# A hybrid decoder block on one core: front, retention and MLP entry in another order

## The chip, the core and the metric

The kernel runs on one core of one Trainium2 chip. The metric is the device time of one execution in microseconds; the times given are medians over several runs. TensorE multiplies (PE, with its weight loads as PEld), VectorE (DVE) and ScalarE (ACT) work element by element, GpSimd (POOL) does small things here, and SyncE (SP) issues nearly all transfers, in order.

## What is computed

One block over 1024 rows of width 1024, in float32:

```python
h = rms_norm(x, g_mix)
qa, ka, va, qr, kr, vr, gr, gate_a, gate_r = split(h @ w_in)
ya = rms_norm(diff_attention(qa, ka, va, lam), g_diff_sub) * (1 - lam_init)  # 8 heads, causal
yr = silu(gr) * rms_norm(retention(qr, kr, vr), g_ret_sub)                   # 4 heads, chunks of 128
mixed = sigmoid(gate_a) * (ya @ w_branch_diff) + sigmoid(gate_r) * (yr @ w_branch_ret)
x = x + mixed @ w_out
x = x + square(relu(rms_norm(x, g_mlp) @ w_ff1)) @ w_ff2
x = x + sigmoid(rms_norm(x, g_ple) @ w_ple_gate) * (p @ w_ple)
out = rms_norm(x, g_final)
```

## The kernel before

Every product is made of float32r parts: split (L119) writes a rounded high part with ACT and the rest with DVE, and three matmuls (high x high, high x low, low x high) go into one PSUM bank. The large projections use a seven-product scheme on 2 x 2 blocks: sums of weight blocks (b11, b21, t1 to t4, b22) meet sums of activation blocks (a11, a12, a22, s1, s2o, s3, s4). unit_prep (L264) is a generator that loads a unit's weights and makes and splits their sums in four steps; product (L299) and product_n (L306) are twelve matmuls each.

Buffers in SBUF go by tags (T0 to T7, S0 to S11, wh, wl, raw, Ga, Gb, o, sq, s2), each with one to three buffers; a new tile of a tag waits until the last reader or writer of the old one is done, a store included. PSUM has eight banks: mm 2, qk 3, sm 2, po 1. A planner orders the instructions of each engine at compile time; the program's order gives the priority. Besides, the program keeps a queue of generators: fill(n) (L213) lets the first one run n steps (six matmuls in a gate or branch), so that independent products lie between dependent ones; drain runs them all.

The stages in order:

- Front. Rows of x are loaded (load_x0, three raw buffers), normed (norm_row), turned by TensorE (row_turned) and split; first_half (L401) takes rows 0 to 3, second_half (L408) rows 4 to 7, where sums of blocks are made too. Between the rows lie the first products of V for attention and retention (v_first, L474, evacuated through the tile s2 by v_spill, L462) and pe_steps (L433), which computes p @ w_ple and stores it in pe_d. v_prep (L483) and v_rest (L505) do the other products of V.
- Twenty units give q and k of both branches and silu(gr), with in_prep (L637) as their unit_prep.
- Retention: for each of four heads ret_qk, ret_kn, ret_scores, ret_chain (eight chunks, one after the other) and ret_turn (L804). One gate's products (gate_steps, L689, 16 steps) lie between, and the queue is drained after each head.
- Attention: 64 tiles (att_tile, L928) of scores, softmax, transposes (turn) and weighing, with PLAN's number of filler steps each: four more gates, the retention's branch products, and at last the first products of the other branch (diff_half). LAST steps follow.
- Output product, rows of x1 and the norm before the MLP: the first 512 columns of all rows, then the other 512 row by row, each row normed, turned and split (lines 1066 to 1133). Here this is called the entry.
- First MLP product: 16 units (ff1_prep, L1142, seven products each) whose outputs and sums go to u_d. Second: PAIRS of products with eight banks, then one pair alone with four banks, while rows are normed for the last stage.
- Last stage: the gate of the per-layer input for two column halves, eight rows each; pe is loaded from pe_d, multiplied and added, then the final norm.

## Time and profile before

| what | value |
|---|---|
| time, median of 3 runs | 1977.43 us (1975.87 to 1980.52) |
| the profiled execution's own time | 1982.06 us |
| its span, first to last instruction | 1980.3 us |
| busy: TensorE, DVE, ACT, POOL | 96%, 66%, 44%, 5% |
| granted TensorE clock, mean | 0.989 |
| DMA | 351.76 MB, 178 GB/s mean |

A busy share is an average over stages with different limits. Matmuls are pipelined, so their durations overlap, and a full stretch is better judged by how many of them it holds. The rows further below show stretches and groups.

### The profile page before, as it was taken

The numbers are of one execution on the slowest core, as the hardware profiler recorded it, in microseconds if no ns is written. First come the engines' busy times: TensorE is split into PE (matmuls) and PEld (weight loads), VectorE is DVE, ScalarE is ACT, GpSimd is POOL, SyncE is SP. The second block draws the span as 40 slices with busy tenths as digits, with TensorE's granted clock in tenths as the row PEclk, the third lists the DMA queues.
The fourth block names the chain that finished last, engine by engine and source line by source line (L and its number), as shares of the span: only waits on it lengthen the run. The fifth ranks groups of instructions, "written<-read, shape, count | busy, mean of one in ns | idle before, by whom it ended". The sixth has DMA issues, their size and how long they took to land.

```text
span 1980.3 us, 24252 instructions
## 1 busy us (share of the span) xinstructions
PE 1906.2 (96%) x8976; PEld 1569.8 (79%) x8976; DVE 1307.5 (66%) x2055; ACT 875.9 (44%) x1385; POOL 96.4 (5%) x112
## 2 busy tenths in 40 slices
PE   8999999999998999999998999799999999999998
PEld 6777788888887878787876887688888878888886
DVE  4777765543466578888886534877677676685754
ACT  6533444334444367666664313433333343333533
POOL 0200000000000011111110000000000000000000
PEclk9999999999999999999998999899999999999999
DMA  8644655532756775588624542254454896563513
GB/s 272 218 157 150 204 174 168 185 118 85 258 195 202 241 195 144 158 267 234 165 92 137 181 149 96 75 176 149 143 172 127 319 375 239 204 232 107 181 38 122
DMA packets 244342, 351.76 MB, mean 178 GB/s; under 512 B 16000, under 2 KB 127744, under 8 KB 242944
## 3 DMA queue, kind: packets, MB, share of 16 engines
q1 hardware_dynamic: 244224, 350.22, 54.9%
q8 instruction: 70, 1.15, 0.2%
q14 instruction: 48, 0.39, 0.1%
HBM read 239.54 MB, written 110.62 MB: 177 GB/s over the span
## 4 chain that ended last, share of the span: by engine, by line
PE 71%; DVE 12%; DMA 7%; ACT 4%; issue 3%; POOL 2%; SPq 1%; POOLq 0%; DVEq 0%; ACTq 0%
PE mm L303 17%; PE qk L303 13%; PE qk L1232 6%; PE mm L186 3%; PE mm L188 3%; PE mm L187 3%; PE mm L1232 3%; PE sm L1232 3%; PE mm L201 2%; PE qk L860 2%; PE mm L202 2%; PE mm L200 2%; PE po L1232 2%; PE mm L311 2%; DVE wl L123 2%
## 5 line engine op out<-in xcount | busy, mean ns | idle before, releaser
L186 PE MATMUL mm<-T,wh 128*128 128x512 f32 x384 | 152.6, 397 | 0.0
L188 PE MATMUL mm<-T,wl 128*128 128x512 f32 x384 | 152.0, 396 | 0.0
L187 PE MATMUL mm<-T,wh 128*128 128x512 f32 x384 | 152.0, 396 | 0.0
L867 ACT ACTIVATE S<-S,stat 128x256 f32<-128x256 f32 (+7 forms) x128 | 98.8, 774 | 36.3 <-DVE stat L862 34.6
L123 DVE TENSOR_TENSOR S<-T,S 128x1024 fp32r<-128x1024 f32 (+1 forms) x46 | 64.7, 1415 | 66.4 <-ACT S L122 66.4
L860 PE MATMUL qk<-S,S 128*128 128x512 f32 (+3 forms) x384 | 101.2, 363 | 2.4 <-DVE stat L862 1.9
L230 POOL TENSOR_TENSOR stat<-stat,mhalf 128x1 f32<-128x1 f32 (+1 forms) x28 | 24.4, 872 | 1437.3 <-DVE stat L228 1437.3
L303 PE MATMUL qk<-T,S 128*128 128x512 f32 x384 | 92.7, 390 | 0.0
L303 PE MATMUL mm<-T,raw 128*128 128x512 f32 x384 | 92.2, 389 | 0.0
L122 ACT CAST S<-T 128x1024 fp32r<-128x1024 f32 (+1 forms) x46 | 54.7, 1203 | 81.4 <-PE qk L303 54.7
L303 PE MATMUL mm<-wh,S 128*128 128x512 f32 x256 | 86.0, 397 | 4.3 <-ACT S L122 4.3
L303 PEld LDWEIGHTS qk<-T,S 128*128 128x128 f32 x384 | 72.4, 188 | 15.1
L303 PEld LDWEIGHTS mm<-T,raw 128*128 128x128 f32 x384 | 72.1, 188 | 15.0
L186 PEld LDWEIGHTS mm<-T,wh 128*128 128x128 f32 x384 | 72.5, 189 | 12.7 <-DVE Ga L991 0.4
L188 PEld LDWEIGHTS mm<-T,wl 128*128 128x128 f32 x384 | 72.3, 188 | 12.9
L187 PEld LDWEIGHTS mm<-T,wh 128*128 128x128 f32 x384 | 72.3, 188 | 12.4
L123 DVE TENSOR_TENSOR S<-sm,S 128x512 fp32r<-128x512 f32 (+2 forms) x116 | 64.4, 571 | 26.2 <-ACT S L122 25.5
L122 ACT CAST S<-S 128x512 fp32r<-128x512 f32 (+2 forms) x52 | 48.3, 950 | 60.7 <-PE qk L303 26.5
L862 DVE CUSTOM_DVE_ANT_0 S<-qk,Gb 128x512 f32<-128x512 f32 (+3 forms) x128 | 72.2, 582 | 3.7 <-ACT Gb L849 2.1
L860 PEld LDWEIGHTS qk<-S,S 128*128 128x128 f32 x384 | 61.4, 189 | 16.3 <-DVE stat L862 10.4
L122 ACT CAST S<-sm 128x512 fp32r<-128x512 f32 (+2 forms) x116 | 54.4, 496 | 44.6 <-PE sm L887 35.0
L122 ACT CAST wh<-S 128x1024 fp32r<-128x1024 f32 (+2 forms) x48 | 54.7, 1158 | 42.6 <-PE po L1232 19.6
(335 smaller groups left out, 4832.0 us busy)
## 6 DMA issues: line engine op xcount, KB each, us to landing
T<-in_w_ff SPq DMA_DIRECT2D x56, 512.0 KB, 5.7
S<-in_w_in SPq DMA_DIRECT2D x52, 512.0 KB, 5.0
S<-qk_d SPq DMA_DIRECT2D x96, 256.0 KB, 5.2
S<-in_w_ff SPq DMA_DIRECT2D x40, 512.0 KB, 6.2
qk_d<-T SPq DMA_DIRECT2D x32, 512.0 KB, 2.9
u_d<-S SPq DMA_DIRECT2D x16, 1024.0 KB, 5.2
u_d<-S SPq DMA_DIRECT2D x16, 768.0 KB, 7.0
T<-u_d SPq DMA_DIRECT2D x24, 512.0 KB, 4.5
```

The lines of the kernel that those rows point to most:

```text
L122: nc.scalar.copy(out=hi, in_=src)
L123: nc.vector.tensor_tensor(out=lo, in0=src, in1=hi.bitcast(F32), op=ALU.subtract)
L186: nc.tensor.matmul(out=ps, lhsT=wh(kt), rhs=ah, start=(kt == 0), stop=False)
L187: nc.tensor.matmul(out=ps, lhsT=wh(kt), rhs=al, start=False, stop=False)
L188: nc.tensor.matmul(out=ps, lhsT=wl(kt), rhs=ah, start=False, stop=(kt == KT - 1))
L200: nc.tensor.matmul(out=ps, lhsT=ah, rhs=wh(kt), start=(kt == 0), stop=False)
L201: nc.tensor.matmul(out=ps, lhsT=ah, rhs=wl(kt), start=False, stop=False)
L303: nc.tensor.matmul(out=ps, lhsT=x[:, k, :], rhs=y[:, k, :], start=(first and k == 0 and n == 0), stop=(k == 3 and n == 2), skip_group_chec ...
L860: nc.tensor.matmul(out=ps, lhsT=qs[:, c, qsl], rhs=kk[:, c, k0:k0 + kw], start=(m == 0), stop=(m == 1))
L862: nc.vector.tensor_tensor_reduce(out=pr[:, c, k0:k0 + kw], in0=ps, in1=bias[0][:, S - w + k0:S - w + k0 + kw], scale=-1.0, scalar=mx[:, 2 ...
L867: nc.scalar.activation(out=pc, in_=pc, func=AF.Exp, scale=-1.0, bias=mx[:, 2 * c + n:2 * c + n + 1], accum_out=z[:, c:c + 1])
L1232: nc.tensor.matmul(out=ps, lhsT=a[x][:, m, k, st * P:(st + 1) * P], rhs=b[y][:, m, k, :], start=(g == 0 and k == 0 and n == 0), stop=(g == ...
```

## The change

The parts, in the program's order:

- pe_steps and pe_d go. The first halves (rows 0 to 3) of gates 4 and 5 are computed in the front as early_gate; their second halves stay in the retention. x rows are loaded ahead of b21; the first products of V take the banks qk, qk, qk, po; rows, products and filler steps stand in another order; va's first two weight sums are made before v_rest (ready).
- in_prep keeps its sums in S2 rather than S3, and b11, b21 in wh.
- Retention: the four gates (48 steps) are queued at once and drained after the last head; the next head's q and k are loaded before ret_scores; ret_turn writes f to o and sq in turn and the high parts to Gb.
- Attention: PLAN and LAST differ, and one filler step may go between the two score groups of a tile.
- Entry: both column halves of w_out are loaded at once; each row gets both halves, is stored to x1_d whole and normed while another half row is multiplied (row_half, row_norm, row_turn). Two of the row's sums go to POOL; s3 and s4 are split once for all rows. The first two products of units 0 and 1 (unit_begin) come before the others, and the weight sums' steps move by one (prep_step). Tags differ throughout, and uy has one buffer.
- The pairs of the second MLP product use other tags. p and w_ple are loaded, turned and split in the last pair's second step, and p @ w_ple is computed in the last stage, six matmuls ahead of each row's product.

```diff
-PLAN = ((2, 2, 2, 2, 2, 2, 2, 2),) * HA
-LAST = 16
+PLAN = ((2, 2, 2, 2, 2, 2, 1, 3),) * (HA - 1) + ((2, 2, 2, 2, 2, 2, 2, 8),)
+LAST = 10
...
-        raw = slot(raw_tag)
+        raw = slot(raw_tag, bufs=2 if raw_tag[0] == "w" else 1)
...
-    pn = slot("T6").rearrange("p (c e) -> p c e", e=DPLE)
-    nc.sync.dma_start(out=pn, in_=t["p"][0, 0].rearrange("(c p) e -> p c e", p=P))
+    load_x0(2)
     b21 = load_b("S1", C_VA, 4)
-    wp = slot("T7")
-    nc.sync.dma_start(out=wp.rearrange("p (k n) -> p k n", k=2), in_=w_block(t["w_ple"][0], 0, D, 0, 2))
-    load_x0(2)
...
-    def pe_steps():
-        wph, wpl = [slot(s, F32R).rearrange("p (k n) -> p k n", k=2) for s in ("S10", "S11")]
...
+    def early_gate(g, raw_tag, tags):
...
         yield
...
+        for u in range(2):
+            yield from t_steps([[a11, a12]], 0, lambda kt: w[0][:, kt, u * P:(u + 1) * P],
+                               lambda kt: w[1][:, kt, u * P:(u + 1) * P],
+                               lambda ps: gate_out(2 * g + u, 0, AF.Sigmoid, ps))
+    def gate_out(unit, half, func, ps):
+        o = slot("Ga", F32, (P, HALF), bufs=2)
+        nc.scalar.activation(out=o, in_=ps, func=func)
+        nc.sync.dma_start(out=gt_d[:, unit, hs(half)], in_=o)
...
-        nw = next(prep)
+        w, nw = ready or [next(prep), next(prep)]
...
-    queue.append(pe_steps())
+    early = [early_gate(4, "T6", ("S6", "S9")), early_gate(5, "T7", ("S10", "S11"))]
+    for g in early:
+        next(g)
+        queue.append(g)
...
     def va_first(i):
-        pb[i] = bank()
+        pb[i] = bank(("qk", "qk", "qk", "po")[i])
         v_first(pb[i], p1a, i, w11)
...
     w21 = split_b(b21)
-    fill(3)
-    v_first(pb[0], p1a, 0, w21, va_d)
     first_half(2)
     va_first(1)
-    fill(3)
+    v_first(pb[0], p1a, 0, w21, va_d)
+    first_half(3)
+    b11 = load_b("S0", C_VR, 0)
+    va_first(2)
     v_first(pb[1], p1a, 1, w21, va_d)
-    first_half(3)
-    b11, b21 = load_b("S0", C_VR, 0), load_b("S1", C_VR, 4)
-    va_first(2)
-    fill(2)
     va_first(3)
-    fill(2)
+    norm_row(4)
     v_first(pb[2], p1a, 2, w21, va_d)
+    b21 = load_b("S1", C_VR, 4)
     a22, s1, s2o = op_tiles("T6", "T7"), op_tiles("S7", "S8"), op_tiles("S4", "S5")
-    norm_row(4)
+    w11 = split_b(b11)
+    fill(4)
+    v_first(pb[3], p1a, 3, w21, va_d)
     second_half(4)
-    w11 = split_b(b11)
-    v_first(pb[3], p1a, 3, w21, va_d)
-    fill(3)
     for st in (5, 6, 7):
         norm_row(st)
+    fill(2)
+    p1r = wide("S3")
+    ps = [bank(("qk", "qk", "qk", "po")[i]) for i in range(4)]
+    va = v_prep(C_VA)
+    v_first(ps[0], p1r, 0, w11)
+    v_first(ps[1], p1r, 1, w11)
     second_half(5)
-    p1r = wide("S3")
     w21 = split_b(b21)
-    va = v_prep(C_VA)
-    for i in range(0, 4, 2):
-        ps = [bank(), bank()]
-        for j in range(2):
-            v_first(ps[j], p1r, i + j, w11)
-        fill(1)
-        second_half(6 + i // 2)
-        for j in range(2):
-            v_first(ps[j], p1r, i + j, w21, vr_d)
-        fill(1)
+    fill(2)
+    for i in (2, 3):
+        v_first(ps[i], p1r, i, w11)
+    second_half(6)
+    fill(2)
+    for i in (0, 1):
+        v_first(ps[i], p1r, i, w21, vr_d)
+    fill(2)
+    second_half(7)
+    next(va)
+    for i in (2, 3):
+        v_first(ps[i], p1r, i, w21, vr_d)
     drain()
-    next(va)
     s3, s4 = op_tiles("S6", "S9"), op_tiles("S10", "S11")
+    ready = []
     for f, (hi, lo) in ((f12, s4), (f11, s3)):
+        ready.append(next(va))
         for k in range(0, 4, 2):
             split(f[:, k:k + 2, :], hi[:, k:k + 2, :], lo[:, k:k + 2, :])
     vr = v_prep(C_VR)
-    v_rest(va_d, p1a, va, lambda: next(vr))
+    v_rest(va_d, p1a, va, lambda: next(vr), ready)
...
-        return unit_prep(w_in, *units[n][0:2], ("S1", "S0")[n % 2], "S3", ("S2", "wh", "wl"))
+        return unit_prep(w_in, *units[n][0:2], ("S1", "S0")[n % 2], "S2", ("wh", "wl", "wh"))
...
+            his = slot("Gb", F32R, (P, 1024)).rearrange("p (a s) -> p a s", a=2)
...
-                f = slot("o", F32, (P, HALF))
+                f = slot(("o", "sq")[half], F32, (P, HALF))
...
-                hi = slot("sq", F32R, (P, HALF))
-                split(f, hi, f.bitcast(F32R))
-                for i, d in enumerate((hi, f.bitcast(F32R))):
+                split(f, his[:, half, :], f.bitcast(F32R))
+                for i, d in enumerate((his[:, half, :], f.bitcast(F32R))):
                     move(yr_d[:, i, h * 2 + e, hs(half)], d)
...
         for c in range(2):
+            if c:
+                fill(between)
...
-            scores(b + 1)
+            m = int(n > 1 and (b + 1) % ST > 3)
+            scores(b + 1, m)
+            n -= m
...
-    gates = iter((4, 5, 6, 7, 0, 1, 2, 3))
+    for g in (4, 5, 6, 7):
+        queue.append(gate_steps(g, AF.Sigmoid, (1,) if g < 6 else (0, 1)))
...
-        queue.append(gate_steps(next(gates), AF.Sigmoid))
         if h == 0:
-            fill(4)
+            fill(2)
...
+        if h + 1 < HR:
+            qk = ret_qk(h + 1)
+            tmp = next(qk)
         sT, rfs = ret_scores(h, qd, kd)
         if h + 1 < HR:
-            v1, qk = ret_v(h + 1), ret_qk(h + 1)
-            tmp = next(qk)
+            v1 = ret_v(h + 1)
...
-        drain()
+    drain()
...
-    wq = [load_quad(w_out, quad, 0) for quad in range(2)]
...
-        run(n_steps(mixed, st, lambda kt: wq[kt // 4][0][:, kt % 4, :], lambda kt: wq[kt // 4][1][:, kt % 4, :], ps))
-        nc.vector.tensor_tensor(out=xa, in0=ps, in1=xa, op=ALU.add)
-        nc.sync.dma_start(out=x1_d[:, st, 0:HALF], in_=xa)
...
+    wq = [[load_quad(w_out, quad, n0, tags[2 * quad:2 * quad + 2] if tags else None) for quad in range(2)]
+          for n0, tags in ((0, None), (HALF, ("S0", "S6", "S7", "S8")))]
...
-    f11, f12 = [slot(s).rearrange("p (k s) -> p k s", k=4) for s in ("S3", "S4")]
-    for st in range(ST):
...
+    f11, f12 = wide("S9"), wide("S10")
+    rows, xns = {}, {}
+    def row_half(st, n):
+        if st not in rows:
+            rows[st] = raw_tile()
+            nc.sync.dma_start(out=rows[st], in_=x_d[st * P:(st + 1) * P, :])
+        ps = bank("qk")
+        run(n_steps(mixed, st, lambda kt: wq[n][kt // 4][0][:, kt % 4, :],
+                    lambda kt: wq[n][kt // 4][1][:, kt % 4, :], ps))
+        add(rows[st][:, hs(n)], ps, rows[st][:, hs(n)])
...
+        row = rows.pop(st)
+        nc.sync.dma_start(out=x1_d[:, st, :], in_=row)
+        xns[st] = slot("Gb", F32, (P, 1024))
         ss = stat()
...
-        f21, f1, f2 = small512("o"), small512("sq"), small512("Ga", 2)
+        f21, f1 = small512("o"), small512("sq")
...
+        add(f1, pt[1], f21)
+        put(f1, s1)
+        add(f1, f1, f11[:, :, cs], ALU.subtract)
+        put(f1, s2o)
         put(pt[1], a22)
-        nc.vector.tensor_tensor(out=f1, in0=pt[1], in1=f21, op=ALU.add)
-        nc.vector.tensor_tensor(out=f2, in0=f1, in1=f11[:, :, cs], op=ALU.subtract)
-        put(f2, s2o)
-        put(f1, s1)
-        nc.vector.tensor_tensor(out=f11[:, :, cs], in0=f11[:, :, cs], in1=f21, op=ALU.subtract)
-        put(f11[:, :, cs], s3)
-        nc.vector.tensor_tensor(out=f12[:, :, cs], in0=f12[:, :, cs], in1=f2, op=ALU.subtract)
-        put(f12[:, :, cs], s4)
+        add(f11[:, :, cs], f11[:, :, cs], f21, ALU.subtract, nc.gpsimd)
+        add(f12[:, :, cs], f12[:, :, cs], f1, ALU.subtract, nc.gpsimd)
...
+    row_half(0, 1)
+    row_half(0, 0)
+    for st in range(4):
+        row_norm(st)
+        row_half(st + 1, 0)
+        row_turn(st)
+        if st < 3:
+            row_half(st + 1, 1)
+    a22, s1, s2o = op_tiles("T0", "T1"), op_tiles("T2", "T3"), op_tiles("S11", "S3")
+    row_half(5, 0)
+    row_half(6, 0)
+    row_half(4, 1)
+    row_norm(4)
+    row_half(7, 0)
+    row_turn(4)
+    row_half(5, 1)
+    row_norm(5)
...
+    def prep_step(u):
+        if u >= UNITS:
+            return
+        if u not in preps:
+            preps[u] = unit_prep(w1, u * P, DFF // 2 + u * P, "wl", "T4", ("wh", "T5", "T6"))
+        opsof[u] = next(preps[u])
+    def unit_begin(u):
...
+        ux = slot(("T7", "S9")[u % 2]).rearrange("p (i s) -> p i s", i=4)
+        pa, pb = bank(), bank("qk")
+        p1 = slot("Ga", F32, (P, HALF), bufs=2)
+        product(pa, ops["b11"], a11, True)
+        nc.scalar.copy(out=p1, in_=pa)
+        product(pb, ops["b21"], a12, True)
+        add(ux[:, 2, :], pb, p1)
+        relu2(ux[:, 2, :])
+        begun[u] = pa, ux
...
-    def ff1_prep(u):
-        return unit_prep(w1, u * P, DFF // 2 + u * P, ("T4", "T5")[u % 2], "T6", ("T7", "S3", "S4"))
...
-    nxt = ff1_prep(0)
-    for _ in range(4):
-        ops = next(nxt)
+    prep_step(0)
+    row_half(6, 1)
+    row_turn(5)
+    row_norm(6)
+    prep_step(1)
+    row_half(7, 1)
+    row_turn(6)
+    row_norm(7)
+    unit_begin(0)
+    row_turn(7)
+    s3, s4 = op_tiles("S0", "S6"), op_tiles("S7", "S8")
+    for f, (hi, lo) in ((f11, s3), (f12, s4)):
+        prep_step(0)
+        for k in (0, 2):
+            split(f[:, k:k + 2, :], hi[:, k:k + 2, :], lo[:, k:k + 2, :])
+    prep_step(0)
+    unit_begin(1)
     for u in range(UNITS):
...
-        ux = slot(("S8", "S10")[u % 2]).rearrange("p (i s) -> p i s", i=4)
-        uy = slot(("S11", "S5")[u % 2]).rearrange("p (i s) -> p i s", i=4)
...
+        if u not in begun:
+            unit_begin(u)
+        now, (pa, ux) = opsof.pop(u), begun.pop(u)
+        uy = slot("S10").rearrange("p (i s) -> p i s", i=4)
...
-        product(pa, now["b11"], a11, True)
...
-        add(ux[:, 2, :], pb, p1)
...
-        ops = next(nxt, None)
+        if u:
+            prep_step(u + 1)
...
-    xs = halves(("S3", "S4", "S6", "S7"))
...
+    xs = halves(("S0", "S6", "S7", "S8"))
...
-    hilo = iter((("S0", "S1", "S2", "S9"), ("wh", "wl", "wh", "wl"), ("T0", "T1", "T2", "T3")) * 8)
-    raws = iter((("T4", "T5"), ("T6", "T7"), ("S5", "S8"), ("S10", "S11")) * 6)
+    hilo = iter((("S4", "S5", "S1", "S2"), ("wh", "wl", "wh", "wl"), ("T0", "T1", "T2", "T3")) * 8)
+    raws = iter((("T7", "T4"), ("S11", "S3"), ("T5", "T6"), ("S9", "S10")) * 6)
+    SIDE = ("S4", "S5", "S10", "S11")
...
+        if g == 1:
...
+            pT = [slot(s, F32R).rearrange("p (k s) -> p k s", k=2) for s in ("S9", "S2")]
...
+            wph, wpl = load_pair(t["w_ple"][0], 0, ("S3", "S1"))
...
-            pe = slot(("o", "sq")[st % 2], F32, (P, HALF))
-            nc.sync.dma_start(out=pe, in_=pe_d[:, st, n0:n0 + HALF])
+            pe = bank("qk")
+            mm = [(a[:, k, ss_], w[:, k, n0:n0 + HALF]) for k in range(2)
+                  for a, w in ((pT[0], wph), (pT[0], wpl), (pT[1], wph))]
+            for i, (l, r) in enumerate(mm):
+                nc.tensor.matmul(out=pe, lhsT=l, rhs=r, start=(i == 0), stop=(i == len(mm) - 1))
```

## Rows read from the trace of the kernel before

**Rows 1.** The page, part 1: busy us (share of span) and instructions of each engine.
```profile
PE 1906.2 (96%) x8976; PEld 1569.8 (79%) x8976; DVE 1307.5 (66%) x2055; ACT 875.9 (44%) x1385; POOL 96.4 (5%) x112
```
**Rows 2.** Busy time by stretch: stretch, length, engines' busy us (instructions), granted clock, DMA share, GB/s.
```profile
2.60:76.00 73.40, 68.42 (x323) 56.28 (x324) 46.03 (x57) 46.49 (x79) 10.94 (x12) 0.95 0.81 275
76.00:112.00 36.00, 28.24 (x118) 21.98 (x117) 26.56 (x31) 18.13 (x27) 6.27 (x4) 0.95 0.52 168
112.00:225.00 113.00, 109.11 (x471) 89.05 (x470) 79.30 (x103) 36.24 (x48) 0.00 (x0) 0.98 0.50 167
225.00:521.50 296.50, 296.50 (x1309) 245.51 (x1309) 158.19 (x207) 116.42 (x164) 0.00 (x0) 1.00 0.48 158
521.50:697.00 175.50, 165.54 (x917) 137.96 (x916) 105.72 (x222) 72.82 (x176) 8.82 (x6) 0.99 0.68 221
697.00:1041.00 344.00, 332.62 (x1818) 272.66 (x1817) 290.85 (x700) 237.93 (x462) 51.13 (x61) 1.00 0.64 179
1202.10:1278.80 76.70, 63.64 (x279) 49.45 (x278) 54.37 (x82) 36.47 (x63) 5.52 (x7) 0.91 0.33 100
1570.00:1600.00 30.00, 28.10 (x123) 22.59 (x122) 13.17 (x10) 7.71 (x6) 0.00 (x0) 1.00 0.98 359
1600.00:1972.00 372.00, 371.77 (x1671) 307.77 (x1669) 242.97 (x248) 143.05 (x150) 9.96 (x15) 1.00 0.52 180
```
**Rows 3.** Timeline of TensorE in the entry: start us, us, what [idle before, its end].
```profile
1193.34 0.39 PE L200 MATMUL mm<-S,T 128*128 128x512 f32 x1
...
1203.14 1.07 PE L1104 MATMUL sm<-ident,Gb 128*128 128x128 f32 x8 [0.58 <-DVE Gb L1096]
1203.97 0.48 PE L201 MATMUL mm<-S,T 128*128 128x512 f32 x1
```
**Rows 4.** Groups, TensorE, 76 to 112 us: count, busy us, mean ns, idle before, releaser.
```profile
L311 PE MATMUL mm<-wh,T 128*128 128x512 f32 x32 | 11.8, 438 | 4.4 <-DVE s L123 4.4
L311 PE MATMUL mm<-wh,S 128*128 128x512 f32 x28 | 9.4, 393 | 3.0 <-DVE s L123 3.0
```
**Rows 5.** Timeline of TensorE at the first unit of the input projection.
```profile
215.42 2.88 PE L303 MATMUL qk<-T,S 128*128 128x512 f32 x12
219.81 0.73 PE L303 MATMUL mm<-S,wh 128*128 128x512 f32 x2 [1.51 <-ACT wh L122]
221.07 1.31 PE L303 MATMUL mm<-S,wh 128*128 128x512 f32 x3 [0.53 <-DVE wh L123]
```
**Rows 6.** Retention, 521.5 to 697: two groups of TensorE, then a row of the waits.
```profile
L810 PE MATMUL sm<-ident,S 128*128 128x128 f32 x64 | 11.9, 283 | 4.5 <-DVE S L801 4.2 <-DVE o L813 0.2
L730 PE MATMUL sm<-ident,S 128*128 128x128 f32 x32 | 4.8, 277 | 1.0 <-DVE o L813 1.0
DVE o L813 <- DMA yr_d<-o: 22.4, 8, 4.7
```
**Rows 7.** Groups, TensorE, 1041 to 1062 us, the end of attention.
```profile
L887 PE MATMUL sm<-ident,S 128*128 128x128 f32 x15 | 3.1, 373 | 6.4 <-DVE S L873 6.4
```
**Rows 8.** Groups, TensorE, 1202.1 to 1278.8 us, the entry.
```profile
L303 PE MATMUL mm<-S,T 128*128 128x512 f32 x24 | 8.7, 511 | 4.9 <-DVE T L123 3.2 <-ACT T L122 1.7
L1104 PE MATMUL sm<-ident,Gb 128*128 128x128 f32 x64 | 8.5, 276 | 3.8 <-DVE Gb L1096 3.8
L303 PE MATMUL mm<-wh,S 128*128 128x512 f32 x8 | 4.7, 657 | 4.3 <-ACT S L122 4.3
```
**Rows 9.** Timeline of DVE and POOL in the front, row 5's sums.
```profile
68.53 0.68 DVE L315 TENSOR_TENSOR sq<-sq,T 128x512 f32<-128x512 f32 x1
...
69.35 1.29 POOL L315 TENSOR_TENSOR T<-T,o 128x512 f32<-128x512 f32 x1 [4.64 <-DVE sq L315]
69.89 1.30 DVE L123 TENSOR_TENSOR S<-sq,S 128x512 fp32r<-128x512 f32 x1 [0.69 <-ACT S L122]
70.60 1.75 POOL L315 TENSOR_TENSOR T<-T,sq 128x512 f32<-128x512 f32 x1
```
**Rows 10.** Waits, 1570 to 1600 us: who for what, us in total, times, longest.
```profile
ACT T L122 <- DMA S<-u_d: 16.9, 1, 16.9
```

117 lines of the change are left out of this document (42 added, 75 removed).

## The prediction

> **What bounds the kernel now.** I read the totals of the page first, then one table of busy time by stage, then in each stage with loss the groups of instructions and what ended the idle time before them. TensorE is busy 1906.2 of 1980.3 us [rows 1], so no other engine's work counts except where TensorE waits for it. The table shows where that is [rows 2]. The twenty units of the input projection (225 to 521.5 us) are full: 1309 products of 512 columns in 296.5 us, which prices one at 0.2265 us. Eight transposes take 0.83 us, from 1203.14 to 1203.97, or 0.104 us each [rows 3]. With these two prices a stage's need is its counts, and the rest is loss:
>
> - 2.6 to 76 us: 227 products and 96 transposes (24 of them the warm-up) need 61.4 of 73.4, loss 12.0, which is the start-up.
> - 76 to 112: 110 and 8 need 25.7 of 36, loss 10.3.
> - 112 to 225: 471 products need 106.7 of 113, loss 6.3.
> - retention, 521.5 to 697: 10.0 idle; attention to 1041: 11.4 idle; at its end 6.4 idle in one place [rows 7].
> - the entry into the MLP, 1202.1 to 1278.8: 215 and 64 need 55.3 of 76.7, loss 21.4, a part of it at the lower clock level (granted clock 0.91, the share at 1.2 GHz), after TensorE had stood idle.
> - start of the second MLP product, 1570 to 1600: 123 need 27.9 of 30, loss 2.1.
> - 1600 to 1972 is full again (371.77 of 372).
>
> So at most some 80 us can be had, and only by giving TensorE something to do in those places.
>
> **The change, part by part.**
>
> The PLE product p @ w_ple leaves the front and goes into the last stage. It is 96 products (2 x 6 for each of eight rows) and 16 transposes (four groups of four in pe_steps): 96 x 0.2265 + 16 x 0.104 = 23.4 us. The last stage is full [rows 2], so all of it is added there. In its place two gates' first halves (2 x 2 chains x 24 = 96 products, 21.7 us) come into the front and leave the retention. TensorE's total does not change: front -1.7, retention -21.7, end +23.4. The transfers of pe_d (16 stores, 16 loads) vanish; they were not waited for on the path. I add 1 us at the end for transposes and weight splits put between full products. The nearest row for such a seam is the 0.5 to 0.6 us that TensorE idles ahead of an inserted transpose [rows 3]; bounds 0 (the stage has DVE to spare) and 4 us.
>
> Front, start-up (loss 12.0): the same first row, constants and weights lead, so I count 0. The PLE products did fill the stretch to 76 us; now the rows themselves must, two products of 12 for each row and block, until the gates may start after row 3. Without 1 MB of p and 1 MB of w_ple ahead of them in SP's queue the third and fourth row come earlier. Bounds: 4 us lost, 2 gained.
>
> Front, 76 to 112 (loss 10.3): TensorE waits 4.4 + 3.0 us for DVE's writes into s2 [rows 4], which is one buffer that waits for its own store to land, while only two mm banks hold products. The change puts the first products into the three qk banks and po, spreads rows 5 to 7 between products and has gate steps ready beside them. I take 7 back; bounds 0 and 9.
>
> Front, 112 to 225 (loss 6.3): at 215.42 twelve products begin and should be followed at 218.14; the next come at 219.81 and, after two, at 221.07, waiting for the split of t2 [rows 5]. That is 1.67 + 0.81 us, and some 1.4 us at the lower clock after it. The cause is in the code: in_prep's sums go to S3, which is p1r, read until the last output of v_rest. Now they go to S2, free long before. With the sums of the V part prepared earlier (ready) I take 3.5; bounds 0 and 5.
>
> Retention: 21.7 us of gate products go, 10.0 us of idle stay in my sum, so 0. For a gain: f alternates between o and sq, and DVE's eight waits for the landing of its own store (22.4 us [rows 6]) should shrink; q and k of the next head are loaded before ret_scores. For a loss: there are 48 gate steps rather than 64 to lie between the head's dependent steps, no drain after each head, and hi now lies in Gb, one buffer that ret_chain's rsp also uses. A wait on it would hold ACT, with the gate's sigmoid, the splits of the next head and so TensorE's banks behind it. TensorE's own idle ahead of the transposes (4.5 us, 4.2 of them for the row scale after the chain's end [rows 6]) is not touched. Bounds: 6 lost, 4 gained, before the rival below.
>
> Attention: one filler step goes between the two score groups, and the plan of steps changes from 2 each to 1 and 3 at a head's end, with 8 in the last tile. Sum of steps: 144 before and after. Of 11.4 us idle I take 1.5; bounds 3 lost, 6 gained. At the end those 6.4 us are a wait for the last probabilities [rows 7]; the added steps need the weights of w_branch_diff, which stand behind the same reload in SP's queue, so 0; bounds 3 lost, 4 gained.
>
> MLP entry (loss 21.4). Two parts of it have different cures. First, while rows are finished, the transposes wait a little each [rows 8]: 3.8 us over eight rows. From the end of row 0's products (1193.34 + 24 x 0.2265 = 1198.78) to its transposes at 1203.14 [rows 3] the norm takes 4.4 us. The new order puts 24 other products (5.4 us) ahead of the transposes, which covers 4.4. Second, at the end nothing is left to do while the last row is normed, turned and split: 4.9 + 4.3 us idle ahead of the units' products [rows 8], and their mean of 511 and 657 ns against the 0.39 us of a product in a full stretch [rows 3] shows the lower clock behind it. The new order keeps unit 0's and unit 1's first two products (2 x 24, 10.9 us) for that gap, and loads and splits unit 0's weights ahead of it. What is late next: DVE has row 7's four splits and sums, the t2 split, the s3 split, each before its product; by about 0.68 us for 512 columns [rows 9] that is some 7 us ahead of t2 against 5.4 us of cover, so 2 us lost there, and up to 1 us a row for rows 4 to 7, whose norms share DVE with the splits of the row before. Four rows hold only three raw buffers, so row 7's load waits for row 4's store; hidden, if its bank may stay full meanwhile. I leave 7 of the 21.4, a gain of 14.5; bounds 8 and 18.
>
> Two of the row's sums move to POOL there. In the front the same two take 1.29 and 1.75 us, and a DVE split that fell beside them took 1.30 us, not 0.68 [rows 9]: 0.6 us of DVE, or 1.2 a row, which the 7 us hold. The Trainium skill ("SBUF — State Buffer", section "SBUF: two separate sides") says more: DVE, with two SBUF inputs, and GpSimd lock a shared port pair for a whole instruction, and the loser fully blocks. By that DVE could stand 1.29 + 1.75 us a row, and the last row's share alone would lie on the path: 3.0 us rather than 1.2 of the entry's gain lost. The row bears out the lock, not its full length.
>
> First MLP product: steady at 19 us a unit and full before. uy becomes one buffer; it is written again some 13 us after its store is issued. 0; bounds 3 lost, 0. Second product's start (2.1): the third pair of raw tiles is no longer the last unit's output, whose store held a load for 16.9 us [rows 10]; gain 1.5; bounds 0 and 2.
>
> Sum: 7 + 3.5 + 1.5 + 14.5 + 1.5 - 1 = 27 us. Against the profiled execution's 1982.06 that is 1955; its median of three is 1977.43, so 1950. The bounds taken together (not all at once) make it 1937 to 1963.
>
> **The rivals.**
>
> A. The retention does not shrink. A head takes 175.5 / 4 = 43.9 us now; my sum needs 38.5. If a head is its own chain of dependent steps (scores, eight chunks, row scale, transposes) rather than TensorE's work, the gate products leave and nothing moves, while the 23.4 us at the end are certain. Price 21.7: 1972. For it: DVE and ACT are only 60% and 41% busy there [rows 2], so latency rules. Against: only 10.0 us were idle, and later steps can be drawn into the gaps.
>
> B. Gb becomes the wait, the side on which the kernel is slower. Per head the second e waits for the first's stores and the next head's rsp for the second's, with the alibi load behind the last: some 12 waits. At the 2.8 us mean of today's eight (22.4 / 8 [rows 6]) that is 34 us if all lie bare: 1984. It decides once 10 of the 12 are bare. For it: ACT waits in order. Against: today's 22.4 us left TensorE no more than 1.2 us idle on that tile (0.2 and 1.0 [rows 6]).
>
> C. The entry's new order does little. The program's order is only a priority for the planner, which already put the transposes into the next row's products [rows 3]; if the last rows' DVE chain is the bound, 14.5 us stay: 1965.
>
> **How the numbers follow.** My forecast 0.62, A 0.16, B 0.10, C 0.12. A change within 0.2% (4 us) can't be told from none here. The forecast gives faster 0.61 and same 0.01; A 0.09 faster, 0.05 same, 0.02 slower; B 0.02 same, 0.08 slower; C 0.11 faster, 0.01 same: faster 0.81, same 0.09, slower 0.10. The range 1936 to 1975 holds the forecast's own, C and most of A.
>
> **What would show it.** Retention some 154 us long, with no ACT wait on Gb's stores; entry with under 8 us of loss and no long stretch at 1.2 GHz; 76 to 112 us without waits for s2; no wait for t2 at the first unit; the last stage 23 to 25 us longer and still full. I am wrong if the retention keeps over 170 us, if TensorE idles over 5 us for rows between the start-up and 76 us, or if the MLP's first unit waits for its split as long as before.

## The result: slower, not faster

| kernel | median of the runs | against before, 95% interval | profiled execution | span |
|---|---|---|---|---|
| before | 1980.5 us (5 runs beside the changed kernel) | 1 | 1982.06 us | 1980.3 us |
| changed | 1994.8 us (5 runs) | 1.0074 (1.0055 to 1.0092) | 1991.08 us | 1988.4 us |

The forecast was 1950 us and faster. The page of the changed kernel, part 1, answers [rows 1]: as many TensorE instructions, of the same kinds, as long busy. So what was lost lies between them.

```profile
PE 1905.5 (96%) x8976; PEld 1571.5 (79%) x8976; DVE 1318.1 (66%) x2047; ACT 871.2 (44%) x1371; POOL 108.2 (5%) x120
```

Busy time by stretch answers [rows 2] (same columns; the stretches are cut where the same work begins and ends):

```profile
2.60:76.00 73.40, 69.26 (x324) 56.86 (x325) 52.36 (x64) 47.72 (x77) 16.89 (x14) 0.95 0.78 250
76.00:112.00 36.00, 33.01 (x142) 26.92 (x141) 26.81 (x31) 14.75 (x19) 3.32 (x2) 0.95 0.44 148
203.50:248.70 45.20, 40.73 (x170) 32.79 (x169) 30.17 (x41) 19.50 (x28) 0.00 (x0) 0.92 0.47 161
515.30:652.30 137.00, 127.84 (x738) 108.39 (x736) 96.69 (x199) 63.31 (x155) 7.29 (x4) 0.98 0.72 233
652.30:1020.60 368.30, 352.48 (x1903) 287.90 (x1902) 302.42 (x724) 244.96 (x479) 52.30 (x63) 1.00 0.66 183
1129.90:1262.00 132.10, 120.13 (x546) 97.41 (x545) 72.58 (x91) 43.54 (x68) 17.12 (x16) 0.99 0.28 93
1544.80:1600.00 55.20, 45.59 (x193) 36.96 (x192) 33.22 (x22) 18.01 (x11) 0.00 (x0) 0.91 1.01 381
```

The reader is to see three things. From 76 to 112 us TensorE does 142 instructions where it did 118. The retention (515 to 652 us) is 137 us long rather than 158.7 (521.6 to 680.3 before). And the start of the second MLP product, which was nearly full, has 45.6 us of work in 55.2 and a granted clock of 0.91.

For the sum a stage's loss is counted more finely than in the prediction: for each TensorE instruction the distance to the next start, less the step that its kind takes in full stretches (0.2267 us for 512 columns, 0.173 for 384, 0.120 for 256, 0.104 for 128, 0.060 for the retention's scores). These steps are those at the full clock, so time at the lower clock counts as loss too. In us, from the two profiled executions:

| stage | before | changed | change | forecast |
|---|---|---|---|---|
| to the first unit | 25.2 | 17.8 | -7.4 | -7 |
| first two units | 4.2 | 7.1 | +2.9 | -3.5 |
| other units and retention, to the first scores | 24.6 | 25.1 | +0.5 | 0 |
| attention, to the last scores | 31.3 | 38.2 | +6.9 | -1.5 |
| attention's end | 11.9 | 11.9 | 0 | 0 |
| branch products after it | 1.6 | 3.3 | +1.7 | 0 |
| entry, w_out to the units | 22.6 | 16.6 | -6.0 | -14.5 |
| first MLP product | 0 | 0 | 0 | 0 |
| second product, its first four pairs | 2.5 | 11.7 | +9.2 | -1.5 |
| rest and last stage | 9.6 | 10.1 | +0.5 | +1 |
| sum | 133.4 | 141.6 | +8.2 | -27 |

The sum is the difference of the spans, 8.1 us. Of the row on the rest and the last stage some 8.7 us lie behind TensorE's last product in either kernel. Between the forecast of -27 and these +8.2 lie 35 us: 10.7 in the second product's start, 8.5 in the entry, 8.4 in the attention, 6.4 in the first units, 1.7 in the branch products. The medians differ by more, 14.3 us: the profiled execution is the fastest of the changed kernel's five, with a granted clock of 0.986 in the mean, and the other four, 3 to 5 us longer, have 0.982 to 0.985. A correction to the text ahead: the input projection has sixteen units (eight of the attention, two times four of the retention), not twenty; the price of a product taken from that stretch is not affected.

How far one execution may be trusted shows where the code of a stage is the same in several kernels below. Entry and branch products together lose 19.9 us in the changed kernel's profile and 19.9 to 27.8, mean 24.4, over the seven profiled executions that have that code unchanged; before it was 24.2, and 24 in d_before_front_dve, whose entry is the same. In the mean over the seven the entry alone loses 3.5 us less than before (6.0 in this one execution) and the branch products 3.4 us more, so that the two together gain nothing. The spread goes with the clock: from the attention's end to the units the changed kernel and c_banks_mm have stops of like length (among them 3.0, 3.6, 4.0 and 2.1 us; 3.2, 3.8, 4.0 and 2.1), but the granted clock of that stretch is 0.99 in the one and 0.95 in the other: over 200 us some 2 us are lost by the clock, over 206 us some 10. The other stages are steadier: first two units 6.1 to 8.0 us, attention 37.5 to 38.5, second product's start 11.4 to 14.4, retention 24.6 to 30.4.

### The profile page after: what moved, and what is told of

Same layout as the page of the kernel before. It is cut to its first block, busy times and chain, and to the rows that moved or that the text cites. A ratio compares the mean times of both kernels' runs of the same rounds, so it can differ in the third digit from the quotient of the medians.

```text
span 1988.4 us, 24138 instructions
## 1 busy us (share of the span) xinstructions
PE 1905.5 (96%) x8976; PEld 1571.5 (79%) x8976; DVE 1318.1 (66%) x2047; ACT 871.2 (44%) x1371; POOL 108.2 (5%) x120
## 3 DMA queue, kind: packets, MB, share of 16 engines
q8 instruction: 70, 1.15, 0.2%
## 4 chain that ended last, share of the span: by engine, by line
PE 69%; DVE 12%; DMA 8%; issue 4%; ACT 4%; POOL 2%; SPq 0%; POOLq 0%; DVEq 0%; ACTq 0%
PE mm L302 17%; PE qk L302 12%; PE qk L1264 5%; PE mm L1264 3%; PE sm L1264 3%; PE mm L187 3%; PE mm L185 3%; PE mm L186 3%; PE qk L853 2%; PE po L895 2%; PE po L1264 2%; DVE wl L122 2%; DVE S L122 1%; PE mm L201 1%; PE mm L200 1%
## 5 line engine op out<-in xcount | busy, mean ns | idle before, releaser
L121 ACT CAST wh<-S 128x1024 fp32r<-128x1024 f32 (+1 forms) x60 | 69.2, 1168 | 107.5 <-PE qk L302 34.6
L302 PE MATMUL mm<-S,T 128*128 128x512 f32 x384 | 92.8, 390 | 2.6 <-DVE S L122 1.9
L302 PE MATMUL mm<-S,wh 128*128 128x512 f32 x384 | 92.5, 390 | 0.0
L302 PE MATMUL qk<-S,wh 128*128 128x512 f32 x384 | 92.4, 389 | 0.0
L302 PEld LDWEIGHTS mm<-S,T 128*128 128x128 f32 x384 | 71.9, 188 | 18.7 <-DVE S L122 2.3
L302 PEld LDWEIGHTS qk<-S,wh 128*128 128x128 f32 x384 | 72.1, 188 | 15.0
L302 PEld LDWEIGHTS mm<-S,wh 128*128 128x128 f32 x384 | 71.8, 188 | 15.1 <-ACT o L656 0.2
L122 DVE TENSOR_TENSOR T<-T,T 128x1024 fp32r<-128x1024 f32 (+1 forms) x24 | 37.6, 1578 | 66.9 <-ACT T L121 66.9
L187 PEld LDWEIGHTS mm<-T,wl 128*128 128x128 f32 x352 | 66.6, 189 | 11.7
L895 PEld LDWEIGHTS po<-S,S 128*128 128x128 f32 x480 | 65.0, 194 | 13.4 <-DVE S L122 7.1
L186 PEld LDWEIGHTS mm<-T,wh 128*128 128x128 f32 x352 | 66.4, 189 | 11.3
```

Source lines behind the costliest of these rows:

```text
L121: nc.scalar.copy(out=hi, in_=src)
L122: nc.vector.tensor_tensor(out=lo, in0=src, in1=hi.bitcast(F32), op=ALU.subtract)
L186: nc.tensor.matmul(out=ps, lhsT=wh(kt), rhs=al, start=False, stop=False)
L187: nc.tensor.matmul(out=ps, lhsT=wl(kt), rhs=ah, start=False, stop=(kt == KT - 1))
L302: nc.tensor.matmul(out=ps, lhsT=x[:, k, :], rhs=y[:, k, :], start=(first and k == 0 and n == 0), stop=(k == 3 and n == 2), skip_group_chec ...
L895: nc.tensor.matmul(out=out, lhsT=v[:, k, :], rhs=a[:, k, q0:256], start=(k == 0 and n == 0), stop=(k == nkt - 1 and n == 2))
```

## The experiments

All are against the kernel before on the same chip, run beside it. The changed kernel was not run again: where a run is compared with it, its 1994.8 us and its ratio of 1.0074 are those of the first comparison. The loss is that of the stage for which the run was made.

| run | median, us | ratio, 95% interval | stage loss, changed kernel to this |
|---|---|---|---|
| a_rows_late | 1983.9 | 1.0011 (0.9994 to 1.0027) | second product's start 11.7 to 0.0 |
| a_p1_gb | 1994.8 | 1.0063 (1.0043 to 1.0084) | first two units 7.1 to 3.2 |
| a_plan_before | 1996.2 | 1.0068 (1.0045 to 1.0091) | attention 38.2 to 38.5 |
| b_turn_last | 1993.2 | 1.0054 (1.0033 to 1.0075) | attention 38.2 to 32.6 |
| b_turn_all | 2016.6 | 1.0178 (1.0159 to 1.0197) | attention 38.2 to 52.3, retention 25.1 to 29.8 |
| a_sums_dve | 1989.4 | 1.0038 (1.0025 to 1.0051) | entry 16.6 to 11.9 |
| b_wq_order | 1994.3 | 1.0058 (1.0037 to 1.0079) | entry and branch products 19.9 to 17.4 |
| b_all | 1963.9 | 0.9913 (0.9895 to 0.9931) | all of these |
| c_all_plan | 1965.1 | 0.9937 (0.9920 to 0.9955) | attention 33.1 (b_all) to 33.0 |
| c_banks_mm | 1997.4 | 1.0102 (1.0078 to 1.0127) | to the first unit 17.8 to 18.1 |
| c_all_front_dve | 1957.7 | 0.9895 (0.9879 to 0.9912) | to the first unit 18.0 (b_all) to 13.2 |
| d_before_front_dve | 1971.8 | 0.9958 (0.9945 to 0.9972) | to the first unit 25.2 (before) to 17.3 |

### The second MLP product: a queue

The changed kernel, TensorE's timeline (start, length, what, in brackets the idle time before and its end), then the waits from 1550 to 1566 us (who for what: total, times, longest), then SP's timeline:

```profile
1554.79 1.07 PE L1264 MATMUL po<-S,S 128*128 128x512 f32 x4
1565.47 0.80 PE L1264 MATMUL mm<-wh,wh 128*128 128x512 f32 x1 [9.61 <-ACT wh L121]
```
```profile
DVE S L1282 <- DMA S<-in_w_ff: 12.5, 1, 12.5
```
```profile
1539.57 3.33 SPq L1227 DMA_DIRECT2D S<-x_d  x5
1548.03 0.37 SPq L1218 DMA_DIRECT2D u_d<-S  x1
1549.83 0.37 SPq L1220 DMA_DIRECT2D u_d<-S  x1
1550.26 3.02 SPq L1227 DMA_DIRECT2D S<-x_d  x3
1553.32 1.10 SPq L1234 DMA_DIRECT2D S<-in_w_ff  x2
```

S3, from which the second weight pair is summed, was s2o, whose last reader is among the first products of the last unit; it is free early. But SP issues in order: rows of x1, which waited 4.4 us for TensorE's reads of the last unit's operands, that unit's two stores, three more rows, and only then S3. The edit, after the products of the first block:

```diff
-    for st in range(ST):
-        nc.sync.dma_start(out=xs(st), in_=x1_d[:, st, :])
...
+            if us == (2, 4) and g == 3:
+                for st in range(ST):
+                    nc.sync.dma_start(out=xs(st), in_=x1_d[:, st, :])
```

> The changed kernel with one move: the eight loads of x1 rows (xs) are no longer issued ahead of the second MLP product but after the fourth of its weight pairs, g == 3 of the first block. Nothing is left out. Theory Q (queue): TensorE's 9.6 us stop at the second pair of raw tiles (S11, S3) is SP's queue: five row loads that wait for the last unit's operands, behind them that unit's two stores, behind them three more row loads, and only then the loads of S3, at 1553.3 us. With the rows later, S3 can be loaded while the last unit still runs; the loss of that stretch falls from 11.7 us to 1 to 3, and the kernel is 8 to 10 us shorter (about 1985 where the changed kernel's median is 1994.8). Rival R: S11 and S3 come free too late whatever stands in the queue, or the stores alone hold it: the loss stays above 6 us and the kernel gains less than 4 us, or the rows, now late, make the first block's last sums wait.

Measured: loss 0.0, and a ratio 0.6% lower, 12 us. SP's timeline of a_rows_late shows the load of S3 15 us sooner, ahead of the last unit's stores:

```profile
1537.81 1.17 SPq L1232 DMA_DIRECT2D S<-in_w_ff  x2
...
1550.51 0.37 SPq L1218 DMA_DIRECT2D u_d<-S  x1
1552.32 0.36 SPq L1220 DMA_DIRECT2D u_d<-S  x1
```

Theory Q holds, with more than it promised: the 2.0 us at the lower clock after the stop went as well.

### The first unit: one wait behind another

The changed kernel, TensorE and then ScalarE at the first unit; it answers [rows 5]:

```profile
213.17 0.49 PE L302 MATMUL mm<-T,wh 128*128 128x512 f32 x1 [1.28 <-ACT wh L121]
216.86 0.79 PE L302 MATMUL mm<-S,wl 128*128 128x512 f32 x1 [3.20 <-ACT Ga L650]
```
```profile
216.22 0.59 ACT L650 COPY Ga<-mm 128x512 f32<-128x512 f32 x1 [3.10 <-DMA vr_d<-Ga]
```

The first line is the second unit's first product, which stops 1.3 us for a split of its weights. t2 is the line below it, at 216.86 and not at 213.17 as the expectation says. t2 (mm<-S,wl) no longer waits for its sums; it waits until its bank's first product is copied to p1, and p1 lies in Ga, out of which the V part's last rows are still being stored.

```diff
-        p1 = slot("Ga", F32, (P, HALF), bufs=2)
+        p1 = slot("Ga", F32, (P, HALF), bufs=2) if n else slot("Gb", F32, (P, 1024))[:, HALF:]
```

> The changed kernel with one buffer changed: the first unit's p1 lies in the free half of Gb rather than in Ga. Theory G: t2's product at 213.17 us no longer waits for t2's sums but for the copy of its own bank into p1, and that copy for Ga, which a last row of the V part is still being stored from (ScalarE idle 3.10 us until the landing in vr_d). With another buffer the wait goes: the loss of the first two units falls from 7.1 us to 2 to 4, the kernel is 3 to 5 us shorter, about 1991. Rival H: o, which u2 of that unit uses and which is stored from in the same way, or DVE's order (two splits of the unit's weights ahead of the last rows' sums) holds the unit as long, and no more than 1 us is won.

Measured: 7.1 to 3.2 us; t2 starts at 208.9. The kernel's time can't tell these 4 us (the intervals overlap). The next wait is already there: t4 stops 2.4 us at 222.5, since DVE's sum for its bank stands behind a subtraction that waits 3.6 us for the second unit's weights. Theory G holds, and the lesson is that this is the third wait in a row at the same place.

### The attention: not the plan, but a table and a queue

> The changed kernel with the attention's order of before: two filler steps in every tile, 16 in the last, none between the two groups of scores. Theory T: the 6.9 us that the attention lost against before (38.2 us of TensorE loss rather than 31.3, by my count of starts against 0.2267 us a product) come from this order: fewer steps lie between the scores and the transposes that wait for the probabilities (17.6 us of waits rather than 8.7). Undone, the stretch goes back to 30 to 33 us of loss and the kernel is 5 to 8 us shorter, about 1988. Rival U: the loss comes from what else runs there (other gates in the queue, another phase of the throttle), and stays above 36 us, with the kernel within 2 us of 1994.8.

(The edit restores PLAN, LAST and att_tile of before.) Measured: 38.5, no change. Theory T falls. A count of the filler products (1536 in gates and branches) that remain as each of heads 0 to 4 begins shows another difference. Before: 1152, 1024, 936, 844, 752. Changed: 1152, 1010, 912, 834, 743. With the plan of before: the same as changed, so the program's number of steps does not decide what TensorE takes. The reason stands in the waits from 646 to 676 us:

```profile
DVE S L855 <- DMA Gb<-in_alibi: 9.7, 1, 9.7
```

and in SP's timeline there: the alibi table goes into Gb, so its load waits for the last head's stores out of Gb:

```profile
653.42 0.93 SPq L88 DMA_DIRECT2D yr_d<-Gb  x2
...
659.88 0.40 SPq L88 DMA_DIRECT2D yr_d<-Gb  x1
660.37 0.41 SPq L88 DMA_DIRECT2D yr_d<-sq  x1
662.79 0.33 SPq L838 DMA_DIRECT2D Gb<-in_alibi  x1
```

Meanwhile TensorE took 14 filler products more, which cost little then (head 0 loses 4.5 us, 3.4 before). In head 4 (9.4 us of loss, 5.3 before) they are missing:

```profile
862.49 0.39 PE L187 MATMUL mm<-T,wl 128*128 128x512 f32 x1
863.37 0.63 PE L880 MATMUL sm<-ident,S 128*128 128x128 f32 x4 [0.49 <-DVE S L866]
...
872.10 0.62 PE L853 MATMUL qk<-S,S 128*128 128x384 f32 x2 [1.65 <-DVE stat L855]
...
877.15 0.40 PE L185 MATMUL mm<-T,wh 128*128 128x512 f32 x1
```
```profile
862.59 0.33 SPq L919 DMA_DIRECT2D ya_d<-o  x1
862.96 1.73 SPq L88 DMA_DIRECT2D S<-qk_d  x3
864.78 1.52 SPq L88 DMA_DIRECT2D S<-va_d  x2
866.35 4.51 SPq L985 DMA_DIRECT2D Ga<-gt_d  x2
```

From 862.7 to 877.2 there is no filler: 696 products remain, 29 chains of 24, so a chain has just ended, and the gates that free the mm banks (L985) stand in SP's queue behind a store that waits and the next head's loads. Before, ten products were left at this place. The edit gives the last head's ret_turn its old buffers:

```diff
+            old = h == HR - 1
-                f = slot(("o", "sq")[half], F32, (P, HALF))
+                f = slot("o" if old else ("o", "sq")[half], F32, (P, HALF))
+                hi = slot("sq", F32R, (P, HALF)) if old else his[:, half, :]
```

> The changed kernel with ret_turn of the last retention head on the buffers of before (f in o, hi in sq; the other heads keep hi in Gb). Theory L: the attention's 6.9 us come from Gb: its first scores need the alibi table, which lies in Gb, and its load stands behind the last head's four stores from Gb (DVE idle 9.67 us until it lands at 669.7 us). Meanwhile TensorE takes filler products from the queue, 142 of 512 columns in head 0 rather than 128, and so stands at the end of a chain 9 products sooner in head 4, where the next gate's load is not issued yet (4.2 of the 6.9 us are lost there, 862 to 877 us). With Gb free the alibi table is loaded before the last head's stores, about 128 filler products go into head 0, and the attention's loss falls from 38.2 to 31 to 34 us; the kernel is 4 to 7 us shorter than 1994.8. Rival M: the last turn's own stores and splits (o is one buffer again) hold the attention's start as long, or the place in head 4 does not depend on the number of products taken; the loss stays above 36 us.

Measured: 1028, 934, 844, 752 products remain as heads 1 to 4 begin, as before within four; head 4 loses 5.5 us, the attention 32.6. Theory L holds for the stage, in b_all, c_all_plan and c_all_front_dve too (32.8 to 33.1). This run's own time does not show it (1.0054, and the interval overlaps that of the changed kernel). In its profile the retention lost 30.4 us; b_all, with the same edit, lost 24.8 there, so the edit does not force that loss.

> The changed kernel with ret_turn of all four heads on the buffers of before. It tells what the new buffers are worth in the retention: from the end of the input projection to the first scores the changed kernel loses about 25.1 us, of which 3.3 us wait for ScalarE's writes into Gb. If the new buffers cost there (rival B of the prediction, in small), this stretch is 1 to 4 us better than with the last head alone undone; if they pay (f alternates and no landing of a store is waited for), it is 1 to 4 us worse. The attention as with the last head alone.

Measured: 2016.6 us, 20 us worse than the changed kernel. The first scores begin at 673.0 rather than 652.3 us, and 70 filler products have been drawn into the retention and are missing in the attention. So the new buffers, and not the smaller number of gate products alone, let the retention shrink: with the old ones DVE waits for each store again:

```profile
DVE o L806 <- DMA yr_d<-o: 15.1, 7, 5.4
```

> The five edits together (1963.9 us), and with them the attention's order of before (two filler steps in every tile, 16 in the last, none between the two groups of scores). Alone on the changed kernel this order moved nothing, but there the filler had run ahead. Theory T2: now that head 0 takes its 128 filler products, the order matters: the attention's loss goes from 33.1 to about 31.3, that of before, or less, and the kernel is 2 us shorter. Rival U2: what the program asks for is not what the engines get, since the planner puts steps where its own times leave gaps; the attention stays at 32 to 34 us of loss and the kernel within 2 us of 1963.9.

Measured: 33.0 us, 1965.1: rival U2. The plan is worth nothing in either place, and as many filler products remain at heads 0 to 4 as in b_all.

### The entry: POOL's sums, and quarters in one buffer

DVE in the changed kernel's entry, groups of one shape (count, busy us, mean ns), then DVE and POOL at row 6:

```profile
L122 DVE TENSOR_TENSOR S<-sq,S 128x512 fp32r<-128x512 f32 x4 | 6.0, 1495 | 0.0
L122 DVE TENSOR_TENSOR T<-sq,T 128x512 fp32r<-128x512 f32 x4 | 2.7, 686 | 0.1
```
```profile
1230.36 1.62 POOL L314 TENSOR_TENSOR S<-S,o 128x512 f32<-128x512 f32 x1 [3.27 <-DVE sq L314]
1230.85 1.67 DVE L279 TENSOR_TENSOR T<-wl,T 128x512 f32<-128x512 f32 x1
1231.93 1.74 POOL L314 TENSOR_TENSOR S<-S,sq 128x512 f32<-128x512 f32 x1
1232.44 1.78 DVE L122 TENSOR_TENSOR S<-sq,S 128x512 fp32r<-128x512 f32 x1
```

The mean of S<-sq,S mixes two cases: the three that began beside a POOL sum took 1.75 to 1.78 us, and row 4's, which began after its sums had ended, took 0.68. Seven of the eight POOL sums of the entry find a DVE instruction beside them and lengthen it by 0.8 to 1.1 us. In the timeline above DVE ends 0.54 and 0.55 us after the POOL sum that it met (1232.52 against 1231.98, 1234.22 against 1233.67), although it began 0.5 us after that sum: it stood until POOL was done. The second POOL sum, in turn, ends 1.15 us after the DVE instruction that it met.

```diff
-        add(f11[:, :, cs], f11[:, :, cs], f21, ALU.subtract, nc.gpsimd)
-        add(f12[:, :, cs], f12[:, :, cs], f1, ALU.subtract, nc.gpsimd)
+        add(f11[:, :, cs], f11[:, :, cs], f21, ALU.subtract)
+        add(f12[:, :, cs], f12[:, :, cs], f1, ALU.subtract)
```

> The changed kernel with the two sums a row of rows 4 to 7 in the entry into the MLP on DVE instead of POOL. Theory P: a DVE instruction beside a POOL sum takes 1.7 to 2.3 us where it takes 0.68 to 1.22 alone; eight such lengthen DVE by about 1 us each, four rows by 8 us, while the sums themselves would cost DVE 8 x 0.68 = 5.4 us. So DVE ends the entry some 2 to 3 us sooner and TensorE's loss there falls from 16.6 us to 13 to 15; the kernel 1 to 3 us shorter. Rival V: the entry waits elsewhere (a norm that started late, row 7's chain), and the loss stays within 1 us of 16.6, or grows by up to 3 us as DVE has more to do.

Measured: the entry's loss is 11.9, below all seven executions with that code unchanged (16.6 to 21.7), the kernel 5 us shorter (1.0038 for 1.0074, the intervals apart). Theory P's outcome came, by more than the 2 to 3 us expected. Its sum is not all of it: DVE was lengthened by 7.1 us and took over 5.4, which is 1.7 us. The planner also gives the instructions another order, and what that brought is not isolated.

> The changed kernel with the four quarters of w_out loaded in another order: both quarters of the second half (into S0, S6, S7, S8) ahead of the first half's second quarter. Theory W: the stop of 3.4 us at 1133.8 us waits for the last quarter of the second half, which the first product of the rows needs; it came late since two of the three raw buffers were held by the first half's second quarter, whose split waits for wh and wl until the branch products end (1129.7 us), so that four loads passed through one buffer, 6.2 us each. In the new order they pass through three buffers. The stop goes, the stretch from the attention's end to the unit products loses 2.5 to 4 us less (19.9 us in the changed kernel), the kernel about 1991. Rival X: the first half's second quarter, now last, takes its place: row 0's first half waits for it, or the rows of x come later, and less than 1 us is won.

(The order of load_quad becomes first half's first quarter, second half's two, first half's second.) Measured: w_out's last quarter is loaded at 1119 to 1121 us, not at 1132.7, and the 3.4 us stop is gone; entry and branch products 17.4 us, under the 19.9 to 27.8 of the unchanged ones. Theory W holds in the trace; the time alone can't tell it.

### Together, and the front

> The changed kernel with five edits together: the x1 rows loaded after the fourth weight pair, the first unit's p1 in Gb, the entry's row sums on DVE, ret_turn of the last head on the buffers of before, the quarters of w_out in the new order. If the causes are separate, the gains add: 12 (second MLP product) + 4 (first units) + 5 (entry) + 5 (attention) + 3 (w_out) = 29 us less than 1994.8, about 1966, faster than the kernel before (1981) by 0.6 to 0.9%. If a wait that is removed only passes the time on to the next one, the sum falls short: 1975 to 1985.

Measured: 1963.9 us, 31 us less than the changed kernel. In ratios the five single runs gain 0.63, 0.11, 0.20, 0.36 and 0.16%, together 1.46%, and b_all 1.61%: the gains add, and the causes are separate. By stage, from its profile: second product's start 11.7 us less, first units 2.3, attention 5.1, entry and branch products 11.4 (19.9 to 8.5); together 30.5, and over all stages 30.0 (141.6 to 111.6).

> The changed kernel with the V part's first products in the two mm banks, as before, rather than in the three qk banks and po. The prediction put the front's gain (76 to 112 us: 10.3 us of loss, mostly waits for DVE's writes into s2) down to these banks and to the gate steps beside them; the changed kernel loses 17.8 us up to its first unit rather than 25.2, with no wait for s2 over 0.4 us. Theory B: the banks carry it; with two mm banks, which the gate steps use too, the waits for s2 come back and the loss up to the first unit is 21 to 25 us, the kernel 3 to 7 us longer than 1994.8. Rival N: the new order (a first product between each pair, no PLE product that needs its own banks) carries it; the loss stays at 17 to 19.5 us and the time within 2 us.

(va_first takes bank() again.) This edit reaches only half of what the expectation says: the four first products of the attention's V. The retention's four stay in the banks qk, qk, qk, po, and the stops for s2 in the kernel before, at 80 and 100 us, stand among those, with s2 stored to vr_d. Measured: 18.1 us to the first unit, no wait for s2 over 0.6 us, and a time that can't be told from the changed kernel's. Rival N for the attention's V: its banks are not what carried the front's gain. For the retention's V this run does not tell; the last run below bears on it.

> The five edits together (1963.9 us), and with them the two sums a row of rows 4 to 7 in the front on DVE instead of POOL, as the entry's already are. Theory P2: beside POOL's sums DVE's splits take up to twice as long in the front too; without them DVE is ahead and the loss up to the first unit falls from 18.0 to 14 to 17 us, the kernel 1 to 3 us shorter. Rival V2: in the front DVE has slack (TensorE waits there for ScalarE's copies into Ga and for one sum), so the loss stays within 1 us of 18.0, or grows by 1 to 3 us since DVE carries 5.4 us more.

(The entry's edit, made in second_half.) Measured: 13.2 us, 1957.7: the fastest. The stretches with the largest holes of the kernel before and of the changed one are full:

```profile
76.00:112.00 36.00, 36.00 (x165) 29.87 (x163) 26.10 (x34) 14.66 (x19) 0.00 (x0) 1.00 0.42 136
1525.00:1580.00 55.00, 55.00 (x244) 45.54 (x243) 34.39 (x22) 20.61 (x13) 0.00 (x0) 1.00 1.01 381
```

> The kernel before, with one edit: the two sums a row of rows 4 to 7 in the front on DVE instead of POOL. In the changed kernel with five edits this took the loss up to the first unit from 18.0 to 13.2 us. Theory P3: the cost is the pair of engines and not the order around it; here too DVE's splits beside POOL's sums are lengthened, TensorE waits for DVE's writes into s2 (3.8 and 3.0 us at 80 and 100 us), and with the sums on DVE the loss up to the first unit falls from 25.2 to 20 to 23 us and the kernel is 2 to 5 us shorter. Rival V3: in the old order those waits are for the landing of a store, which no engine's speed moves; the loss stays within 1 us of 25.2 and the time within 2 us.

Measured: 17.3 us rather than 25.2, a kernel 0.42% faster by two lines changed. The outcome of theory P3 came: the pair of engines costs, in the old order too. And all eight first products are in the two mm banks here, so that few banks alone do not make the stops for s2. TensorE's waits for s2 in either kernel, before and with the sums on DVE, then ScalarE in the kernel before:

```profile
PE mm L311 <- DVE s L123: 7.4, 3, 3.8
PE mm L311 <- DVE s L123: 1.1, 1, 1.1
```
```profile
82.69 0.59 ACT L122 CAST s<-mm 128x512 fp32r<-128x512 f32 x1 [2.15 <-DMA vr_d<-s]
```

What the pair costs by is not settled, and it is not only P3's lengthened splits: within the stop of 3.8 us that ends at 84.7 us ScalarE, which writes s2 first, waits 2.15 us for the landing of s2's store, as rival V3 had it. Three things more are in the trace. DVE's own busy time does not fall. In the kernel before the two sums of row 6 keep POOL until 87.1 us, and the next row's first copy into o, which they read, starts at 91.2; with DVE they end at 81.1. And the planner, with other engines, turns the next row ten us sooner. No run separates them.

## Why the prediction was wrong, point by point

- Second product's start, +9.2 for -1.5: the failed step is "the third pair of raw tiles is no longer the last unit's output". True, but only tiles were followed, not the queue that loads them. The second pair moved to tiles whose load stands behind eight row loads and two stores. The prediction had [rows 10] in hand, where a store held a load, and did not ask which loads now stood behind which stores. Shown by a_rows_late.
- First units, +2.9 for -3.5: the t2 wait went, as said. The failed step is that nothing was counted behind it; "what is late next" was asked for the entry and not here. It was Ga's store. Shown by a_p1_gb.
- Attention, +6.9 for -1.5: the failed step is that the term was put on PLAN, which does nothing. The alibi load was named in rival B ("with the alibi load behind the last") as one wait in twelve, but its price was taken as idle time where it lies; most of it was paid 200 us later in head 4. Shown by b_turn_last, for 5.6 us, 3.9 of them in head 4 (9.4 to 5.5).
- Entry, -6.0 in the profile and -3.5 in the mean over seven, for -14.5: the mechanism was right in part; the failed step is the size of POOL's term. It was put at 0.6 us per sum from one row [rows 9]; the entry shows 0.8 to 1.1, and 4.7 us of loss go with the sums. And w_out's second half was taken as loaded in time (a stop of 3.4 us). With both mended the entry loses 6.8 us (b_all), close to the 7 that the sum left. Rival C ("does little") is what happened, though not for its reason.
- Branch products, +1.7, and +3.4 in the mean: put at nothing. Most of it is one stop of 2.9 us that ends at 1072.6 us, where TensorE waits for ScalarE's split of the attention's last output; w_out's quarters are not the cause, as their first load is issued at 1080.9. No run isolates it, so the cause stays open.
- Front, -7.4 for -7: right number, wrong reason. It named the banks and the gate steps; c_banks_mm says no for half of the banks, and in d_before_front_dve the stops for s2 all but go with the old banks and without gate steps, a like gain by taking POOL out alone. So the hit is luck in part. What the new order itself brought was not isolated.
- Retention, +0.5 for 0: right. The stretch shrank by 21.7 us, the price of 96 gate products; rival A is false, though b_turn_all shows that it would have been true with the old buffers. Of rival B's waits, ScalarE stood 3.4 us for the stores out of Gb and TensorE 3.0 us for ScalarE's writes into it, not 34.
- Last stage, -0.2 for +1, with the PLE product's 23.4 us on the path as said.

On the rule of the Trainium skill ("SBUF — State Buffer", section "SBUF: two separate sides"), by which a DVE instruction with two SBUF inputs and a GpSimd instruction that reads SBUF exclude each other for a whole instruction: the trace agrees, in size too. DVE's instructions at row 6 of the entry end 0.54 and 0.55 us after the POOL sums that they met. The prediction read its own row [rows 9] wrongly when it said that the row bears out the lock but not its full length: that split ends at 71.19, 0.55 us after the sum that ends at 70.64. It was only 0.6 us longer because it began 0.54 us after the sum did. So the price is what is left of the sum when DVE comes, 0.5 to 1.1 us in the front of the kernel before and in the changed kernel's entry, and POOL stands for DVE in the same way. A split with one input in PSUM did not stand: in the kernel before s<-mm,s at 96.37 us took 0.68 us in the middle of a POOL sum. The truth lay between the prediction's 1.2 us a row and its 3.0, at 1.8 (7.1 us over four rows), and the consequence, that those sums should not be on POOL, was not drawn.

## What to carry over

A new order of buffers is also a new order of each in-order queue: write down, for every load that moved, what stands before it on its issuing engine and what that waits for. When a wait is removed, look for the next one on the same buffer or bank, since here two waits passed the loss on. A stage that fills gaps from a shared stock of products pays for an early delay later, where the stock runs out.

## What was not expected of the hardware

Two subtractions a row, 1.3 to 2.3 us each on an engine that is busy 5% of the time, cost more on POOL than on DVE at 0.68 us each: 8 of them made the kernel before 0.42% slower, and the loss to the first unit 8 us larger, although DVE looks like the fuller engine (66%). Where the two meet on SBUF they stand for each other to the end of the instruction, and DVE's busy time counts that standing (1.78 us for 0.68). And runs of one kernel differ by 4 to 14 us here between the lowest and the highest; the entry with the branch products varies by 8 us from one profile to another with the same code and like stops, at granted clocks of 0.95 to 0.99.
